# The tail of a two-layer decoder trunk: row factors with one tensor input, products of rows on GpSimd, scaling on VectorE

## The chip, the cores and the metric

The kernel runs on one core of a Trainium2 chip. The metric is the device time of one execution in microseconds; a median of three runs is given, and one further execution was recorded by the hardware profiler. Lower is better.

## The reference, cut to what matters

The program is a decoder trunk of two layers for 512 positions of 1024 features, in float32. Both layers are a mixer and a gated feed-forward block, each behind an RMS norm and added to the residual. After the second feed-forward block comes a last RMS norm:

```python
def rms_norm(x, g):
    x32 = x.astype(jnp.float32)
    y = x32 * lax.rsqrt(jnp.mean(x32 * x32, axis=-1, keepdims=True) + EPS)
    return y.astype(x.dtype) * g
...
    h = h + gated_conv_ffn(hn, w_ffn_gate[layer], w_ffn_up[layer], conv_ffn[layer],
                           b_conv_ffn[layer], w_ffn_down[layer])
return rms_norm(h, final_norm)
```

Only the end matters here: the last part of the down projection of layer 1, the residual `y` that it is added to, and the last norm, which scales each position by a factor of its own and each feature by `final_norm`.

## The kernel before, in words

Matrices in float32 are multiplied as three products of split operands (a high and a low part). In the body of the kernel activations lie with features on the partitions; in the last down projection that turns round, and the output is built as four *rows*: tiles `y[0]` to `y[3]` of 128 positions by 1024 features, each with a left and a right half of 512 features.

The tail is the end of the function `ffn1`. The last four blocks of hidden features are multiplied with their weights by a scheme of seven block products in place of eight (numbers 1 to 7; products 1, 2, 3 and 6 belong to rows 0 and 1, products 5, 7 and 4 to rows 2 and 3). Sums of products share PSUM banks: 1, 6, 7 and 4 go on top of each other in bank "a", 5 and 3 in bank "e", 2 has bank "b"; a product that goes on top of another may start only when VectorE has read the sum so far. The last product of all, number 2 for row 1, is made in two parts of 256 columns in banks "c" and "d".

From `taken(1, 0, left)` on, the order in which VectorE, ScalarE and GpSimd work is written out by hand, line by line: each call is bound to program order (`inorder`), and each engine works through its own instructions in that order. The calls are:

- `taken` (its add has line 1104, its matmuls 1204): makes a block product on TensorE and adds it on VectorE to a half of `y`, times the factor of the feed-forward norm. Inputs of the add: PSUM, a column, `y` in SBUF.
- `squared` (1221): ScalarE squares a half of `y` and writes the sum of squares of each position into a column of `ssf` (an ACTIVATE and a read-out of the accumulator).
- `halved` (1227 for the first half, 1229 for the next): VectorE collects the sums of a row, times -0.5/1024, in another column of `ssf`.
- `rooted` (1232): ScalarE takes the square root.
- `inverted` (1236 to 1238): VectorE takes the reciprocal and improves it by one Newton step of two instructions; the result is the row's factor, one number per position.
- `times` (1241): the product of a half of `y` with `final_norm` (the tile `fin`), on VectorE or GpSimd, into `yf`. It doesn't need the factor.
- `scaled` (1245 on ScalarE, 1246 on GpSimd or VectorE): multiplies `yf` by the factor into `y`, and issues the store of that half (1247; 256 KB), on the queue of SP or, for row 1 right, of ScalarE.
- The last: row 1 left is multiplied by factor and `final_norm` in one VectorE instruction (1307) and stored (1309).

The rows are finished in the order 0, 2, 3, 1. Before the change GpSimd has four instructions in this part: the product of row 2 right, the scaling of row 2 right, the product of row 3 left, the scaling of row 3 left. VectorE makes the other products, except that of row 1 left, which is in the last instruction.

Of the kernel before, what the change touches and what calls it, by code (L numbers as in the profile page):

```python
# [12 lines left out]
ALU = mybir.AluOpType  # L13
# [3 lines left out]
D = 1024  # L17
# [5 lines left out]
EPS = 1e-6  # L23
# [8 lines left out]
def tile_trunk(ctx: ExitStack, tc: tile.TileContext, x, norm_mix, norm_ffn, final_norm,  # L32
# [19 lines left out]
    inorder = tc.keep_in_program_order  # L52
# [1026 lines left out]
    def ffn1(norm):  # L1079
        with tc.tile_pool(name="f1", bufs=1) as ap:  # L1080
# [20 lines left out]
            left, right = slice(0, 512), slice(512, D)  # L1101

            def add(dst, ps, t):
                return nc.vector.scalar_tensor_tensor(dst, ps, ffn.cols[:, t : t + 1], dst,  # L1104
                                                      op0=ALU.mult, op1=ALU.add)
# [86 lines left out]
            def product(p, i, c0=0, c1=512, bank=None):  # L1192

                at = bank or BANK[p], i
                first = at not in banks
                if first:
                    banks[at] = mm_bank(f"dn{a}_{at[0]}{i}")
                ps = banks[at][:, c0:c1]
                cs = slice(i * P, (i + 1) * P)
                (l_hi, l_lo), (r_hi, r_lo) = blocks[p], stat[p]  # L1200
                for k in range(2):
                    for l, r, end in ((l_hi, r_hi, False), (l_hi, r_lo, False),
                                      (l_lo, r_hi, k == 1)):
                        nc.tensor.matmul(ps, l[:, k, cs], r[:, k, c0:c1], start=first, stop=end,
                                         skip_group_check=True)
                        first = False
                return ps

            vec, act, pool = nc.vector, nc.scalar, nc.gpsimd
# [3 lines left out]
            def taken(p, i, cs, bank=None):  # L1213

                t = i + 2 * (p in (5, 7, 4))
                part = cs if bank else slice(0, 512)
                inorder(add(y[t][:, cs], product(p, i, part.start, part.stop, bank), t))

            def squared(t, cs):
                sq = tp.tile([P, S], F32, tag="sq", name=f"sqf{t}_{cs.start}")  # L1220
                inorder(act.activation(sq[:, : cs.stop - cs.start], y[t][:, cs], AF.Square,
                                       accum_out=ssf[:, t, cs.start // 256 : cs.start // 256 + 1]))

            def halved(t, cs, first):

                ss, ms = ssf[:, t, cs.start // 256 : cs.start // 256 + 1], ssf[:, t, 3:4]
                inorder(vec.tensor_scalar(ms, ss, -0.5 / D, -0.5 * EPS, op0=ALU.mult, op1=ALU.add)
                        if first else
                        vec.scalar_tensor_tensor(ms, ss, -0.5 / D, ms, op0=ALU.mult, op1=ALU.add))

            def rooted(t):
                inorder(act.activation(root[t], ssf[:, t, 3:4], AF.Sqrt, scale=-2.0))

            def inverted(t):
                ms, r = ssf[:, t, 3:4], factor[t]
                inorder(vec.reciprocal(r, root[t]))
                inorder(vec.scalar_tensor_tensor(ms, ms, r, r, op0=ALU.mult, op1=ALU.mult))
                inorder(vec.scalar_tensor_tensor(r, ms, 1.5, r, op0=ALU.add, op1=ALU.mult))

            def times(engine, t, cs):  # L1240
                inorder(engine.tensor_tensor(rows_f[t][:, cs], y[t][:, cs], fin[:, cs], ALU.mult))

            def scaled(engine, t, cs, queue=nc.sync):
                dst, src, r = y[t][:, cs], rows_f[t][:, cs], factor[t]
                inorder(act.activation(dst, src, AF.Copy, scale=r) if engine is act else
                        engine.tensor_scalar(dst, src, r, None, op0=ALU.mult))
                queue.dma_start(out[t * P : (t + 1) * P, cs], dst)
# [6 lines left out]
            squared(0, left)  # L1254
            times(vec, 0, left)
            halved(0, left, True)
            taken(6, 0, right)
            taken(6, 1, right)
            taken(3, 0, right)
            squared(0, right)  # L1260
            times(vec, 0, right)
            taken(7, 0, right)
            halved(0, right, False)
            rooted(0)
            squared(2, right)
            times(pool, 2, right)
            inverted(0)
            taken(7, 1, right)
            scaled(act, 0, left)
            scaled(act, 0, right)  # L1270
            halved(2, right, True)
            taken(4, 0, left)
            squared(2, left)
            times(vec, 2, left)
            halved(2, left, False)
            rooted(2)
            taken(5, 1, right)
            squared(3, right)
            inverted(2)
            taken(4, 1, left)  # L1280
            scaled(act, 2, left)
            scaled(pool, 2, right)
            halved(3, right, True)
            times(vec, 3, right)
            times(pool, 3, left)
            squared(3, left)
            taken(3, 1, right)
            squared(1, right)
            halved(3, left, False)
            rooted(3)  # L1290

            first, second = slice(0, 256), slice(256, 512)
            taken(2, 1, first, "c")
            squared(1, first)
            halved(1, right, True)
            taken(2, 1, second, "d")
            squared(1, second)
            inverted(3)
            scaled(pool, 3, left)
            times(vec, 1, right)  # L1300
            halved(1, first, False)
            halved(1, second, False)
            rooted(1)
            scaled(act, 3, right)
            inverted(1)
            scaled(act, 1, right, nc.scalar)
            inorder(vec.scalar_tensor_tensor(y[1][:, left], y[1][:, left], factor[1],
# [4 lines left out]
    n = ffn0(n)  # L1312
    n = mixer1(n)
    ffn1(n)


# [28 lines left out]
```

## Time and profile before

| | |
|---|---|
| median of 3 runs | 988.8 us (988.59 to 989.36) |
| the profiled execution | 988.85 us |
| its span | 987.1 us |
| granted TensorE clock, mean | 0.998 |
| last matmul of the kernel starts | 977.52 us |
| last instruction on VectorE (line 1307) | 981.68 us, 0.75 us long |
| stores of the output | 8 of 256 KB, seven on SP's queue, one on ScalarE's |

The span runs from the first to the last event in the profile; all times of the trace count from its start. In the timeline each row has its start, its length, engine, line of the kernel, operation, and output <- inputs with their shapes; a bracket names the idle time before it and what ended that. VectorE's instructions overlap a little: the next one that depends on nothing begins somewhat ahead of the end that the row shows. In the chain of waits a row has start, length, engine, tile and line.

### The profile page before, as it was taken

The numbers are of one execution on the slowest core, as the hardware profiler recorded it, in microseconds if no ns is written. First come the engines' busy times: TensorE is split into PE (matmuls) and PEld (weight loads), VectorE is DVE, ScalarE is ACT, GpSimd is POOL, SyncE is SP. The second block draws the span as 40 slices with busy tenths as digits, with TensorE's granted clock in tenths as the row PEclk, the third lists the DMA queues.
The fourth block names the chain that finished last, engine by engine and source line by source line (L and its number), as shares of the span: only waits on it lengthen the run. The fifth ranks groups of instructions, "written<-read, shape, count | busy, mean of one in ns | idle before, by whom it ended". The sixth has DMA issues, their size and how long they took to land.

```text
span 987.1 us, 15485 instructions
## 1 busy us (share of the span) xinstructions
PE 975.2 (99%) x6099; PEld 879.9 (89%) x6099; DVE 775.9 (79%) x1181; ACT 562.0 (57%) x843; POOL 112.0 (11%) x129
## 2 busy tenths in 40 slices
PE   9999999999999999999999999999999999999996
PEld 6788888999999999999889988889999999999985
DVE  5797458998788887886887765589987779777787
ACT  5623347755465654655488734576655456554675
POOL 2142022000000000000210001210000000000022
PEclk9999999999999999999999999999999999999999
DMA  7442225555465454653324623264565465445573
GB/s 248 131 150 85 86 86 128 135 137 157 129 150 133 132 142 129 150 130 108 126 64 120 198 69 106 55 140 128 150 166 133 130 149 147 119 135 135 161 151 116
DMA packets 87942, 129.32 MB, mean 131 GB/s; under 512 B 4309, under 2 KB 57789, under 8 KB 87869
## 3 DMA queue, kind: packets, MB, share of 16 engines
q1 hardware_dynamic: 78172, 98.69, 32.2%
q0 software_dynamic: 8208, 27.79, 15.5%
q10 hardware_dynamic: 1488, 1.84, 0.6%
q8 instruction: 48, 0.79, 0.3%
q14 instruction: 26, 0.20, 0.1%
HBM read 98.42 MB, written 2.10 MB: 102 GB/s over the span
## 4 chain that ended last, share of the span: by engine, by line
PE 85%; DVE 8%; ACT 2%; issue 1%; DMA 0%; POOL 0%; ACTq 0%; DVEq 0%
PE dn L153 3%; PE dn L154 3%; PE dn L155 3%; PE d L153 3%; PE d L154 3%; PE d L155 3%; PE oo L155 1%; PE oo L153 1%; PE oo L154 1%; PE oe L154 1%; PE oe L153 1%; PE oe L155 1%; PE u_20a L542 1%; PE u_18a L542 1%; PE u_16a L542 1%
## 5 line engine op out<-in xcount | busy, mean ns | idle before, releaser
L576 DVE SCALAR_TENSOR_TENSOR c<-rows,prm,c 128x512 f32<-128x512 f32 x88 | 64.1, 747 | 1.5 <-ACT c L574 1.4
L140 POOL DMA_DIRECT2D wlo_g<-raw_g x20 | 17.2, 859 | 387.4 <-ACT wlo_g L139 350.4
L153 PE MATMUL d<-a_hi,whi_d 128*128 128x512 f32 x144 | 56.1, 390 | 0.0
L153 PE MATMUL dn<-whi_dn,a_hi 128*128 128x512 f32 x144 | 56.1, 390 | 0.0
L154 PE MATMUL dn<-wlo_dn,a_hi 128*128 128x512 f32 x144 | 56.1, 390 | 0.0
L154 PE MATMUL d<-a_lo,whi_d 128*128 128x512 f32 x144 | 56.1, 390 | 0.0
L155 PE MATMUL d<-a_hi,wlo_d 128*128 128x512 f32 x144 | 56.0, 389 | 0.0
L155 PE MATMUL dn<-whi_dn,a_lo 128*128 128x512 f32 x144 | 56.0, 389 | 0.0
L679 DVE TENSOR_TENSOR wlo_s34u<-s34u,whi_s34u 128x1024 fp32r<-128x1024 f32 x20 | 24.5, 1224 | 25.5 <-ACT whi_s34u L678 25.5
L149 DVE TENSOR_TENSOR wlo_dn<-raw_dn,whi_dn 128x1024 fp32r<-128x1024 f32 x18 | 22.0, 1225 | 23.6 <-ACT whi_dn L148 23.4
L142 ACT ACTIVATE whi_u<-raw_u 128x1024 fp32r<-128x1024 f32 x21 | 22.2, 1055 | 31.6 <-PE d L154 17.5
L149 DVE TENSOR_TENSOR wlo_d<-raw_d,whi_d 128x1024 fp32r<-128x1024 f32 x18 | 22.0, 1224 | 19.5 <-ACT whi_d L148 19.5
L198 ACT ACTIVATE hgh<-h,prm 128x512 fp32r<-128x512 f32 x24 | 17.3, 722 | 35.1 <-DVE h L309 35.0
L140 POOL DMA_DIRECT2D wlo_u<-raw_u x21 | 18.1, 860 | 162.0 <-ACT wlo_u L139 83.7
L584 ACT ACTIVATE s<-c,prm 128x512 f32<-128x512 f32 x44 | 31.2, 714 | 7.3 <-DVE c L576 7.2
L209 POOL TENSOR_TENSOR ssq_f<-ssq_f,sq_f 128x512 f32<-128x512 f32 x14 | 19.7, 1410 | 132.3 <-ACT sq_f L208 97.5
L260 ACT ACTIVATE a_hi<-s 128x512 fp32r<-128x512 f32 x40 | 25.0, 626 | 15.7 <-PE dn L154 9.9
L199 DVE SCALAR_TENSOR_TENSOR hgl<-h,prm,hgh 128x512 fp32r<-128x512 f32 x24 | 23.2, 965 | 12.0 <-ACT hgh L198 11.9
L155 PEld LDWEIGHTS d<-a_hi,wlo_d 128*128 128x128 f32 x144 | 27.0, 188 | 5.7
L155 PEld LDWEIGHTS dn<-whi_dn,a_lo 128*128 128x128 f32 x144 | 27.0, 188 | 5.7
L1104 DVE SCALAR_TENSOR_TENSOR y<-dn,small,y 128x512 f32<-128x512 f32 x40 | 27.7, 748 | 5.5 <-PE dn L155 5.5
L153 PEld LDWEIGHTS d<-a_hi,whi_d 128*128 128x128 f32 x144 | 27.1, 188 | 5.3
(1489 smaller groups left out, 3762.7 us busy)
## 6 DMA issues: line engine op xcount, KB each, us to landing
raw_g<-in_w_ffn_gate_dram SPq DMA_DIRECT2D x40, 512.0 KB, 3.8
raw_u<-in_w_ffn_up_dram SPq DMA_DIRECT2D x40, 512.0 KB, 3.7
raw_dn<-in_w_ffn_down_dram SPq DMA_DIRECT2D x22, 512.0 KB, 3.6
wlo_u<-raw_u POOLq DMA_DIRECT2D x21, 512.0 KB, 5.7
wlo_g<-raw_g POOLq DMA_DIRECT2D x20, 512.0 KB, 4.6
raw_d<-in_w_ffn_down_dram SPq DMA_DIRECT2D x18, 512.0 KB, 3.7
raw_oe<-in_w_out_even_dram SPq DMA_DIRECT2D x8, 512.0 KB, 3.6
raw_v<-in_w_in_odd_dram SPq DMA_DIRECT2D x8, 512.0 KB, 4.5
```

The costliest lines, as they stand in the source:

```text
L140: nc.gpsimd.dma_start(lo, raw, accum_op=ALU.add)
L149: behind(nc.vector.tensor_tensor(lo, raw, hi.bitcast(F32), ALU.subtract), after[0])
L153: nc.tensor.matmul(ps, lhs[0], rhs[0], start=start, stop=False)
L154: nc.tensor.matmul(ps, lhs[0], rhs[1], start=False, stop=False)
L155: nc.tensor.matmul(ps, lhs[1], rhs[0], start=False, stop=stop)
L199: nc.vector.scalar_tensor_tensor(hg[k][1], h[k], g, hg[k][0].bitcast(F32), op0=ALU.mult, op1=ALU.subtract)
L260: nc.scalar.activation(hi, src, AF.Copy, scale=scale)
L542: nc.tensor.matmul(ps, l, r, start=first, stop=end, skip_group_check=True)
L576: nc.vector.scalar_tensor_tensor(c, t[:, i : S + i], prm("cf", i * NF + ft), c, op0=ALU.mult, op1=ALU.add)
L584: nc.scalar.activation(s, c, AF.Silu, bias=self.prm("bf", ft))
L679: nc.vector.tensor_tensor(lo, src, hi.bitcast(F32), ALU.subtract)
L1104: return nc.vector.scalar_tensor_tensor(dst, ps, ffn.cols[:, t : t + 1], dst, op0=ALU.mult, op1=ALU.add)
```

## The change

The columns and the order of the tail are changed, and nothing ahead of it.

- `halved` for the second sum of a row, and both instructions of the Newton step, become `tensor_scalar`: one tensor input of 128x1, and what was the second tensor input is now a scalar operand, a column with one number per partition. The arithmetic is the same.
- Row 2: GpSimd makes both products; ScalarE scales the right half, VectorE the left. Before, VectorE and GpSimd made one product each, ScalarE scaled the left half and GpSimd the right.
- Row 3: GpSimd makes both products; VectorE scales the left half, GpSimd the right. Before, VectorE and GpSimd made one each, GpSimd scaled the left half and ScalarE the right.
- Row 1: GpSimd makes the product of the right half, in place of VectorE. The left half is squared in one instruction of 512 columns and not two of 256, so that there are two sums for the row and not three.
- The order of calls moves with that. Row 3's factor is worked out between the two adds of row 1 left, and row 3's scaling comes ahead of row 1's last sum. On TensorE one matmul of the last product (bank "c") now stands ahead of product 3 of row 1; all else there is as before.

On GpSimd there are now six instructions: the products of row 2 right, row 2 left, row 3 right, row 3 left and row 1 right, then the scaling of row 3 right. The stores keep their order on SP's queue by rows (0, 2, 3, then 1 left), with row 2's right half ahead of its left one as before. Within row 3 the order as the scheduler writes it is the right half (GpSimd's) and then the left (VectorE's); before the change it was the left (GpSimd's) and then the right (ScalarE's). Lines of the changed kernel from 1229 on stand one lower up to 1246 (the sums are all line 1227, the Newton step 1235 to 1237, products 1240, scalings 1244 and 1245), and the last instruction is line 1303.

```diff
--- before.py
+++ after.py
@@ -1224,9 +1224,8 @@
             def halved(t, cs, first):
 
                 ss, ms = ssf[:, t, cs.start // 256 : cs.start // 256 + 1], ssf[:, t, 3:4]
-                inorder(vec.tensor_scalar(ms, ss, -0.5 / D, -0.5 * EPS, op0=ALU.mult, op1=ALU.add)
-                        if first else
-                        vec.scalar_tensor_tensor(ms, ss, -0.5 / D, ms, op0=ALU.mult, op1=ALU.add))
+                inorder(vec.tensor_scalar(ms, ss, -0.5 / D, -0.5 * EPS if first else ms,
+                                          op0=ALU.mult, op1=ALU.add))
 
             def rooted(t):
                 inorder(act.activation(root[t], ssf[:, t, 3:4], AF.Sqrt, scale=-2.0))
@@ -1234,8 +1233,8 @@
             def inverted(t):
                 ms, r = ssf[:, t, 3:4], factor[t]
                 inorder(vec.reciprocal(r, root[t]))
-                inorder(vec.scalar_tensor_tensor(ms, ms, r, r, op0=ALU.mult, op1=ALU.mult))
-                inorder(vec.scalar_tensor_tensor(r, ms, 1.5, r, op0=ALU.add, op1=ALU.mult))
+                inorder(vec.tensor_scalar(ms, ms, r, r, op0=ALU.mult, op1=ALU.mult))
+                inorder(vec.tensor_scalar(r, ms, 1.5, r, op0=ALU.add, op1=ALU.mult))
 
             def times(engine, t, cs):
                 inorder(engine.tensor_tensor(rows_f[t][:, cs], y[t][:, cs], fin[:, cs], ALU.mult))
@@ -1271,37 +1270,34 @@
             halved(2, right, True)
             taken(4, 0, left)
             squared(2, left)
-            times(vec, 2, left)
+            times(pool, 2, left)
             halved(2, left, False)
             rooted(2)
             taken(5, 1, right)
             squared(3, right)
+            times(pool, 3, right)
             inverted(2)
             taken(4, 1, left)
-            scaled(act, 2, left)
-            scaled(pool, 2, right)
+            scaled(act, 2, right)
             halved(3, right, True)
-            times(vec, 3, right)
+            scaled(vec, 2, left)
             times(pool, 3, left)
             squared(3, left)
             taken(3, 1, right)
-            squared(1, right)
+            times(pool, 1, right)
             halved(3, left, False)
             rooted(3)
-
-            first, second = slice(0, 256), slice(256, 512)
-            taken(2, 1, first, "c")
-            squared(1, first)
+            squared(1, right)
+
+            taken(2, 1, slice(0, 256), "c")
+            inverted(3)
+            taken(2, 1, slice(256, 512), "d")
+            squared(1, left)
             halved(1, right, True)
-            taken(2, 1, second, "d")
-            squared(1, second)
-            inverted(3)
-            scaled(pool, 3, left)
-            times(vec, 1, right)
-            halved(1, first, False)
-            halved(1, second, False)
+            scaled(vec, 3, left)
+            scaled(pool, 3, right)
+            halved(1, left, False)
             rooted(1)
-            scaled(act, 3, right)
             inverted(1)
             scaled(act, 1, right, nc.scalar)
             inorder(vec.scalar_tensor_tensor(y[1][:, left], y[1][:, left], factor[1],
```

## The prediction

> **What bounds the kernel now.** The page's list of busy time comes first, to see where the change can matter at all.
>
> ```profile
> span 987.1 us, 15485 instructions
> PE 975.2 (99%) x6099; PEld 879.9 (89%) x6099; DVE 775.9 (79%) x1181; ACT 562.0 (57%) x843; POOL 112.0 (11%) x129
> ```
>
> TensorE (PE) fills nearly the whole span, and the edit leaves its work alone but for one matmul that moves. So only the tail can change, where TensorE runs out of products. The second view is the chain that ended last, cut to the end.
>
> ```profile
> 970.62 0.86 DVE ssf L1237
> ...
> 977.28 0.95 DVE ssf L1229
> ...
> 979.60 0.60 DVE yf L1241
> ...
> 980.38 0.40 DVE ssf L1229
> ```
>
> Its last 14 us are VectorE (DVE) nearly throughout. Two of its pieces, 0.86 and 0.95 us, are instructions on one number per partition. The third view, the timeline, says why.
>
> ```profile
> 970.17 1.29 POOL L1241 TENSOR_TENSOR yf<-y,fin 128x512 f32<-128x512 f32 x1 [7.03 <-DVE ssf L1229]
> ...
> 970.42 0.16 DVE L1236 RECIPROCAL ssf<-ssf 128x1 f32<-128x1 f32 x1 [0.27 <-ACT ssf L1232]
> ...
> 970.62 0.85 DVE L1237 SCALAR_TENSOR_TENSOR ssf<-ssf 128x1 f32<-128x1 f32 x1
> ...
> 975.39 1.57 POOL L1246 TENSOR_SCALAR y<-yf,ssf 128x512 f32<-128x512 f32 x1 [3.93 <-DVE ssf L1238]
> ...
> 975.76 0.14 DVE L1227 TENSOR_SCALAR ssf<-ssf 128x1 f32<-128x1 f32 x1
> ...
> 976.54 0.74 DVE L1104 SCALAR_TENSOR_TENSOR y<-dn_e,small,y 128x512 f32<-128x512 f32 x1
> ...
> 976.94 1.27 POOL L1241 TENSOR_TENSOR yf<-y,fin 128x512 f32<-128x512 f32 x1
> ...
> 977.20 1.03 DVE L1229 SCALAR_TENSOR_TENSOR ssf<-ssf 128x1 f32<-128x1 f32 x1
> ```
>
> L1237 started 0.45 us into a GpSimd (POOL) product and ended with it (971.47 against 971.46); L1229 likewise (978.23 against 978.21). Both read two SBUF tensors. What did not wait beside GpSimd reads one: the reciprocal (0.16), L1227 (0.14), and L1104, whose other tensor is in PSUM (0.74).
>
> After the last VectorE instruction come the stores. The windows of 0.25 us show their transfers (last two columns: DMA share, GB/s).
>
> ```profile
> 982.25:982.50 0.25, 0.00 (x0) 0.00 (x0) 0.18 (x1) 0.15 (x1) 0.00 (x0) 0.78 0.11 41
> 982.50:982.75 0.25, 0.00 (x0) 0.00 (x0) 0.00 (x0) 0.00 (x0) 0.00 (x0) 0.50 0.95 360
> ...
> 985.25:985.50 0.25, 0.00 (x0) 0.00 (x0) 0.00 (x0) 0.00 (x0) 0.00 (x0) 0.50 0.15 49
> ```
>
> Transfers run without a gap from about 982.47 to 985.29: four of 256 KB, 0.70 us each. They are row 3's two halves and row 1's two, the first of them row 3 left: SP's queue, which takes its stores in order, had it waiting until GpSimd had scaled it (981.63, below). From the last byte to the end of the span are 1.81 us, and from the span to the time of this execution (988.85) 1.75; both I leave as they are. The execution is 0.05 over the median, 988.8.
>
> **The change, step by step.** More rows carry the terms.
>
> ```profile
> 971.60 0.39 PE L1204 MATMUL dn_a<-whi_dnp,hgl 128*128 128x512 f32 x1
> ...
> 972.30 0.74 DVE L1104 SCALAR_TENSOR_TENSOR y<-dn_a,small,y 128x512 f32<-128x512 f32 x1
> ...
> 974.32 0.39 PE L1204 MATMUL dn_a<-whi_dnp,hgl 128*128 128x512 f32 x1
> 974.71 0.19 PEld L1204 LDWEIGHTS dn_e<-whi_dnp,hgh 128*128 128x128 f32 x1 [0.43 <-DVE y L1104]
> ...
> 975.97 0.39 PE L1204 MATMUL dn_e<-whi_dnp,hgl 128*128 128x512 f32 x1
> ...
> 977.37 0.63 ACT L1221 ACTIVATE sqf<-y 128x512 f32<-128x512 f32 x1 [0.67 <-DVE y L1104]
> ...
> 977.91 0.19 ACT L1221 ACTIVATION_READ_ACCUMULATOR sqf<-y 128x1 f32 x1
> ...
> 978.61 0.47 DVE L1104 SCALAR_TENSOR_TENSOR y<-dn_d,small,y 128x256 f32<-128x256 f32 x1
> ...
> 979.80 1.83 POOL L1246 TENSOR_SCALAR y<-yf,ssf 128x512 f32<-128x512 f32 x1 [1.59 <-ACT sqf L1221]
> 980.12 0.65 DVE L1229 SCALAR_TENSOR_TENSOR ssf<-ssf 128x1 f32<-128x1 f32 x2
> ...
> 981.23 0.22 DVE L1237 SCALAR_TENSOR_TENSOR ssf<-ssf 128x1 f32<-128x1 f32 x1
> 981.48 0.16 DVE L1238 SCALAR_TENSOR_TENSOR ssf<-ssf 128x1 f32<-128x1 f32 x1
> 981.68 0.75 DVE L1307 SCALAR_TENSOR_TENSOR y<-y,ssf,fin 128x512 f32<-128x512 f32 x1
> 982.43 0.39 ACTq L1247 DMA_DIRECT2D out_dram<-y  x1
> ```
>
> *The small steps.* With one tensor input they should no longer wait for GpSimd. In the rows a small step that needs the one before it starts 0.03 after that one's end (981.45 to 981.48), a big add 0.66 after the add ahead of it. No row has a 128x1 TENSOR_SCALAR with a column as scalar. L1237, which has one, takes 0.22, L1238 without 0.16: so a column is worth 0.06. Bounds are 0.14 (L1227) and 0.28 (two columns at 0.06 more); I take 0.22 for every one, which costs 0.06 twice in each row's chain.
>
> *Row 0.* L1237's wait of 0.63 (0.85 for 0.22) goes. With a column in the sum ahead the reciprocal starts at 970.48, the steps at 970.67 and 970.92, and the next add, of row 3 left, which waits for none of them, at 971.03: 0.55 earlier (the 0.63, less 0.06 for the sum's column and some 0.02 of spacing). Then TensorE is late: the product for row 2 left ends at 971.60 + 0.39 = 971.99, so that add starts at 972.03 (972.30 before). Of 0.55, 0.27 is left.
>
> *Row 2.* VectorE's product of row 2 left goes to GpSimd, which is idle there. VectorE gains nothing at once, as the sum waits for ScalarE (ACT): the square starts at 972.80, its read-out ends 0.73 later (977.37 to 978.10 in the row), the sum runs 973.56 to 973.77. The add of row 3 right ends at 974.44. TensorE, which waited 0.43 for that add, also has one narrow matmul of the last product to run ahead of it now; product 3 starts at 974.67 for 974.71 and, as it no longer breaks at its start, ends at 976.19 for 976.36.
>
> *Row 2 scaled on VectorE.* The form is known from the first mixer, alone and beside a GpSimd product:
>
> ```profile
> 71.59 0.49 DVE L270 TENSOR_SCALAR cv<-rows,prm 128x512 f32<-128x512 f32 x1
> ...
> 74.31 1.04 DVE L270 TENSOR_SCALAR cv<-rows,prm 128x512 f32<-128x512 f32 x1
> ```
> ```profile
> 73.79 1.29 POOL L498 TENSOR_TENSOR cv<-cv,rstd_m 128x512 f32<-128x512 f32 x1 [9.88 <-PE av L155]
> ```
>
> It takes 0.49 alone, and ends 0.27 after the product (75.35 against 75.08) where it has to wait. Here it is asked for at 975.66 (behind row 2's small steps and row 3's left add, which starts at 974.93, plus 0.66, plus 0.07 for a small sum), GpSimd's product of row 3 right runs 974.53 to 975.81, so it ends at 976.09: before product 3 does. Hidden, with 0.1 us to spare.
>
> *Row 3.* The add of row 1 right starts at 976.23 (976.54), row 3's sum 0.66 later and ends at 977.10, where L1229 ended at 978.23: 1.13 us. Root to 977.33, reciprocal to 977.56, two steps: the factor is there at 978.05 (979.60, where the product behind it starts in the chain). The last add, behind the second step, starts at 977.97 for 978.61.
>
> *Row 1.* The two 256-wide squares become one 512-wide: 978.47 to the read-out's end at 979.20 (a price of 0.2). The product of row 1 right (L1241, 0.60 of the chain) is off VectorE, one sum is gone, and the sum of 0.40 that waited beside GpSimd's scaling is free: it runs 979.23 to 979.44, where it ended at 980.77. Then root (0.20), reciprocal (0.16) and two steps (0.22), each with its 0.03: the factor at 980.37, the last instruction 980.40 to 981.15, against 981.68 to 982.43. That is 1.28 us.
>
> *Stores.* SP's queue takes them in its own order. By the order of the instructions row 3 right, which GpSimd scales, now stands ahead of row 3 left, which VectorE scales: so row 3 left, ready at 978.8, waits behind GpSimd, and the last burst has four transfers again. GpSimd scales row 3 right after its product of row 1 right (977.24 to 978.52, behind that of row 3 left, 976.09 to 977.24: 1.27 less a start that the wait covers) and VectorE's scaling of row 3 left (to 978.8); its two rows give 1.57 and 1.83, the second with some 0.4 behind a VectorE product, so I take 1.5: ready at 980.3, against 981.63 for the store that opened the burst before. First bytes come some 0.85 after that (982.47 for 981.63): 981.15. Four transfers of 0.70 end at 983.97. Row 1's stores, issued 0.75 and some 0.8 after the last instruction starts (981.68 to 982.43 before), so at 981.13 and 981.2, have first bytes due at 981.98 and 982.05, and their turns come at 982.55 and 983.25: they have slack of 0.57 and 1.2. So of VectorE's 1.28 nothing reaches the end by itself; what counts is that GpSimd is done 1.33 earlier, thanks to work ahead of it that came earlier or went.
>
> Sum: span 987.1 - 1.3 = 985.8, plus 1.75 makes 987.5. The price of a column does not enter (slack). GpSimd's scaling does, at full: at 1.83 the time is 987.9, at 1.2 (the shortest that I hold possible without a VectorE product beside it, from its 1.57 with one) 987.2. Products at 1.15 for 1.28 would give 0.4 more. So 986.8 to 987.9.
>
> **The Trainium skill, weighed.** Its page "SBUF — State Buffer", section "Who interferes with whom", says that VectorE and GpSimd hold their common pair of ports for a whole instruction, and that `tensor_scalar` may take it in its two-port mode; the L270 row agrees (1.04 for 0.49). Read widely, that speaks against the edit, for the small steps become `tensor_scalar` too; L1227 (0.14 beside GpSimd) is against the wide reading. By the narrow one the sum is 987.5, by the wide one that of the third rival. The section also says that the order of issue decides who waits; it agrees with the rows under the first rival.
>
> **Rivals.** *First: GpSimd gets ahead at a hand-over.* Twice a VectorE scaling waits out a GpSimd product with another GpSimd instruction queued: asked for at 975.66 and 978.43, with the products ending at 975.81 and 978.52. If GpSimd goes on, the scaling, and all VectorE queued behind it, wait for one instruction more.
>
> ```profile
> 55.79 3.47 POOL L484 TENSOR_TENSOR ac<-ac,rstd_m 128x512 f32<-128x512 f32 x2 [0.70 <-DVE pl L464]
> ```
> ```profile
> 56.93 1.19 DVE L262 TENSOR_TENSOR pl_lo<-pl,pl_hi 128x512 fp32r<-128x512 f32 x1
> 58.03 1.78 DVE L456 TENSOR_TENSOR zs<-zs 128x521 f32<-128x521 f32 x1
> ```
>
> Two queued GpSimd products: the VectorE one at 56.93 came in about half a microsecond late, the next waited some 1.1. So VectorE got in between the two. But the margins, 0.15 and 0.09, are the size of my errors. Lost at the second place, GpSimd's scaling is done 0.3 earlier, but row 1's last sum starts at 980.25, 1.0 late: row 1's stores are issued at 982.15, their transfers end at 984.4, time 987.9. Lost at the first, the add of row 1 right starts at 977.26, GpSimd then reaches the second place first too, and row 1's sum starts at 981.15: the last instruction ends at 983.1, the last byte near 985.3, as before: 988.8.
>
> *Second: the products on GpSimd take longer there.* Four follow each other from 972.86 and one scaling.
>
> ```profile
> L484 POOL TENSOR_TENSOR ac<-ac,rstd_m 128x512 f32<-128x512 f32 x4 | 9.7, 2443 | 22.7 <-ACT pl_hi L260 19.0 <-DVE ac L483 3.0 <-DVE pl L464 0.7
> ```
>
> At 2.44 us each the scaling ends at 972.86 + 9.8 + 1.5 = 984.1, or 984.7 with two waits of 0.28 for VectorE. All four transfers follow: 984.7 + 0.85 + 2.8 + 1.81 = 990.2, with 1.75 a time of 991.9, slower than before. It decides where the scaling ends after 981.63, from 1.7 us a product on; from 2.2 the loss passes 0.2%. Against it: L484 ran beside VectorE work on two SBUF tensors; the tail's adds read one, and GpSimd took 1.27 beside one.
>
> *Third: the change doesn't do what it says; the small TENSOR_SCALARs wait too.* Then row 2's factor waits for the product that ends at 975.81, row 3's sum and second step for the next two, row 1's for GpSimd's scaling: the last instruction ends near 984.0, and the time is about 989.7.
>
> **How the numbers follow.** Forecast 0.64, 987.5; second place lost 0.12, 987.9; first place lost 0.08, 988.8; long products 0.10, 988.9 to 991.9; small steps waiting 0.06, 989.7. The range 986.7 to 989.0 holds the first three, the edges of the forecast's own 986.8 to 987.9 included, and the beginning of the fourth. What a measurement here can tell from no change is about 0.2%, 2.0 us: faster by that means under 986.8, the edge of the forecast's case, a quarter of it if I allow for what GpSimd's rows are worth: 0.18. Over 990.8 come only products above 2.2 us: 0.06. Within: 0.76.
>
> **What would show it.** Right: no 128x1 VectorE row over 0.3 us; TENSOR_SCALAR 128x512 on VectorE ends some 0.3 us after a GpSimd product, and before the next; TensorE without its 0.43 us gap; the last burst of four transfers opened by row 3 right, at some 0.85 us behind the end of GpSimd's scaling, with row 1's last instruction long done. Wrong: small rows that end with GpSimd's; GpSimd products well above 1.3 us; GpSimd's scaling of row 3 right ahead of VectorE's of row 3 left; a burst of three.

## The result, and the profile after

| | before | after |
|---|---|---|
| median | 989.09 us (20 runs, 988.49 to 990.14) | 987.58 us (20 runs, 987.10 to 988.79) |
| profiled execution, its span | 988.85, 987.1 | 987.73, 986.0 |

The ratio is 0.9985, with a 95% interval of 0.9979 to 0.9992: faster, by 1.5 us. That is 0.15%, less than the 0.2% that the prediction thought a measurement needed. Forecast were 987.5 and 1.3 us.

First VectorE's rows of the kernel after, from the timeline (start, length, engine, line):

```profile
970.75 0.28 DVE L1236 TENSOR_SCALAR ssf<-ssf 128x1 f32<-128x1 f32 x1
...
974.63 0.27 DVE L1236 TENSOR_SCALAR ssf<-ssf 128x1 f32<-128x1 f32 x1
...
975.78 0.48 DVE L1245 TENSOR_SCALAR y<-yf,ssf 128x512 f32<-128x512 f32 x1
976.32 0.75 DVE L1104 SCALAR_TENSOR_TENSOR y<-dn_e,small,y 128x512 f32<-128x512 f32 x1
976.99 0.20 DVE L1227 TENSOR_SCALAR ssf<-ssf 128x1 f32<-128x1 f32 x1
...
978.58 0.48 DVE L1245 TENSOR_SCALAR y<-yf,ssf 128x512 f32<-128x512 f32 x1
979.46 0.21 DVE L1227 TENSOR_SCALAR ssf<-ssf 128x1 f32<-128x1 f32 x1 [0.40 <-ACT sqf L1221]
...
980.70 0.75 DVE L1303 SCALAR_TENSOR_TENSOR y<-y,ssf,fin 128x512 f32<-128x512 f32 x1
```

and GpSimd's in the same stretch:

```profile
974.60 4.05 POOL L1240 TENSOR_TENSOR yf<-y,fin 128x512 f32<-128x512 f32 x3 [0.37 <-DVE ssf L1235]
978.63 1.87 POOL L1245 TENSOR_SCALAR y<-yf,ssf 128x512 f32<-128x512 f32 x1
```

GpSimd is busy from 974.60 to 980.50 without a break, and no small VectorE step beside it takes over 0.28 us; before, two had taken 0.85 and 1.03. GpSimd's last row is 1.87 long where it takes 1.57 alone (e6): it waited for VectorE's scaling. Row 3's sum (976.99) ends at 977.19, where it had ended at 978.23. Both scalings on VectorE (0.48 each) ran as if alone.

The windows of 0.25 us show the last burst (last two columns DMA share and GB/s):

```profile
981.25:981.50 0.25, 0.00 (x0) 0.00 (x0) 0.20 (x1) 0.25 (x1) 0.00 (x0) 1.00 0.47 180
981.50:981.75 0.25, 0.00 (x0) 0.00 (x0) 0.00 (x0) 0.00 (x1) 0.00 (x0) 0.61 1.05 385
...
984.00:984.25 0.25, 0.00 (x0) 0.00 (x0) 0.00 (x0) 0.00 (x0) 0.00 (x0) 0.50 0.63 221
984.25:984.50 0.25, 0.00 (x0) 0.00 (x0) 0.00 (x0) 0.00 (x0) 0.00 (x0) 0.50 0.10 41
```

Four transfers again. A window counts a packet where it starts; by the single packets of the trace they run from 981.37 (0.86 after GpSimd's scaling) to 984.38, and then it is 1.64 us to the end of the span (before: to 985.42, then 1.72). And here is the chain that ended last, as the profile draws it:

```profile
979.71 0.21 ACT ssf L1231
...
980.45 0.23 DVE ssf L1237
...
980.78 0.72 ACT y L1244
```

It runs through row 1's factor to ScalarE's last scaling and does not know GpSimd or the queue of stores. The prediction said that these last instructions have slack and that GpSimd's scaling sets the end.

Chain and timeline also leave out the closing instructions of the program. The view of the program's last line lists them; these are its rows for GpSimd's DRAIN, an instruction that GpSimd runs three times there, before and then after (shortest, median and longest in ns, then where the first and the last start):

```profile
L1341 POOLq DRAIN  x3: 34/93/6617, 979.8 to 986.9; - x3
```
```profile
L1337 POOLq DRAIN  x3: 34/102/6862, 978.4 to 985.8; - x3
```

The longest of the three is the first. By the trace's records, after the change it ends at 985.24, 4.74 us after GpSimd's last instruction; before it ended at 986.37, also 4.74 after. SP, which waits for the stores to land, is through at 985.03 (before: 986.33), and the span ends at 986.02 (987.13): both times 0.77 after the DRAIN. So there are two ways by which GpSimd's scaling can reach the end, the stores behind it and this DRAIN. Which of them counts, and that the drawn chain does not, the experiments show.

### The profile page after: what moved, and what is told of

The parts are those of the page before. It is cut to its first block, busy times and chain, and to the rows that moved or that the text cites. A ratio compares the mean times of both kernels' runs of the same rounds, so it can differ in the third digit from the quotient of the medians.

```text
span 986.0 us, 15484 instructions
## 1 busy us (share of the span) xinstructions
PE 974.6 (99%) x6099; PEld 879.9 (89%) x6099; DVE 772.8 (78%) x1179; ACT 560.8 (57%) x840; POOL 115.1 (12%) x131
## 4 chain that ended last, share of the span: by engine, by line
PE 86%; DVE 7%; ACT 3%; issue 2%; DMA 1%; POOL 0%; ACTq 0%; DVEq 0%
PE dn L154 3%; PE dn L153 3%; PE dn L155 3%; PE d L154 3%; PE d L153 3%; PE d L155 3%; PE oo L155 1%; PE oo L154 1%; PE oo L153 1%; PE oe L155 1%; PE oe L154 1%; PE oe L153 1%; PE u_20a L542 1%; PE u_16a L542 1%; PE u_14a L542 1%
```

## The experiments

The tail begins earlier or later from one execution to the next (from 968.84 in e5 to 970.57 in e6), so places in it are compared as distances from one event, the mark: the start of VectorE's add of row 2's first right half (line 1104; 969.34 before, 969.42 after), ahead of which no kernel differs. The first five columns of numbers are worked out so from the traces, in us. "Stores landed" is where SP is through with its waits for the stores, "DRAIN ends" is GpSimd's. The last two columns are the measured medians against the kernel before on the same chip.

| kernel | GpSimd's scaling ends | last VectorE instruction starts | stores landed | DRAIN ends | end of span | median (before) | ratio (95%) |
|---|---|---|---|---|---|---|---|
| before | 12.29 | 12.34 | 16.99 | 17.03 | 17.80 | | 1 |
| after | 11.09 | 11.28 | 15.62 | 15.83 | 16.60 | 987.58 (989.09) | 0.9985 (0.9979 to 0.9992) |
| e1: small steps alone | 11.88 | 11.92 | 16.57 | 16.62 | 17.38 | 988.46 (989.44) | 0.9989 (0.9980 to 0.9998) |
| e2: all but the small steps | 12.80 | 13.33 | 17.32 | 17.54 | 18.30 | 989.46 (989.44) | 1.0003 (0.9994 to 1.0011) |
| e3: other order of stores | 11.01 | 11.28 | 15.16 | 15.75 | 16.52 | 987.76 (989.44) | 0.9985 (0.9976 to 0.9994) |
| e4: one product twice | 12.32 | 11.28 | 17.30 | 17.07 | 18.05 | 989.60 (989.44) | 1.0001 (0.9992 to 1.0010) |
| e5: row 3 all on VectorE | none | 11.28 | 15.16 | 13.96 | 15.90 | 987.16 (989.37) | 0.9976 (0.9967 to 0.9985) |
| e6: e3, two squares | 10.77 | 11.31 | 15.04 | 15.51 | 16.27 | 987.48 (989.37) | 0.9982 (0.9973 to 0.9990) |
| e7: GpSimd first | 10.77 | 11.71 | 15.59 | 15.51 | 16.34 | 987.34 (989.37) | 0.9979 (0.9970 to 0.9988) |
| e8: e1, sum later | 11.57 | 11.62 | 16.27 | 16.32 | 17.08 | 988.27 (989.37) | 0.9989 (0.9980 to 0.9998) |
| e9: after, again | 11.08 | 11.28 | 15.61 | 15.82 | 16.59 | 987.74 (989.15) | 0.9986 (0.9977 to 0.9995) |
| e10: e5, again | none | 11.28 | 15.17 | 13.96 | 15.92 | 987.00 (989.15) | 0.9979 (0.9970 to 0.9988) |
| e11: row 3 right on ScalarE, two squares | none | 11.11 | 14.75 | 13.97 | 15.50 | 986.37 (989.15) | 0.9973 (0.9963 to 0.9984) |

The last instruction on VectorE stands at 11.28 in six rows, to the hundredth: the distances repeat far better than the medians, whose intervals are some 0.9 us to each side. Two things hold in every row. The DRAIN ends 4.74 after GpSimd's last instruction (in e5, e10 and e11 that is a product, which ends at 9.22 or 9.23). The span ends 0.75 to 0.77 after the later one of stores and DRAIN. That is the DRAIN in the kernel before, the changed kernel, e1, e2, e3, e6, e8 and e9, by 0.04 to 0.59; in e4, e5, e7, e10 and e11 it is the stores.

### e1 and e2: the two halves of the change

e1 is the kernel before with this alone:

```diff
-                inorder(vec.tensor_scalar(ms, ss, -0.5 / D, -0.5 * EPS, op0=ALU.mult, op1=ALU.add)
-                        if first else
-                        vec.scalar_tensor_tensor(ms, ss, -0.5 / D, ms, op0=ALU.mult, op1=ALU.add))
+                inorder(vec.tensor_scalar(ms, ss, -0.5 / D, -0.5 * EPS if first else ms,
+                                          op0=ALU.mult, op1=ALU.add))
...
-                inorder(vec.scalar_tensor_tensor(ms, ms, r, r, op0=ALU.mult, op1=ALU.mult))
-                inorder(vec.scalar_tensor_tensor(r, ms, 1.5, r, op0=ALU.add, op1=ALU.mult))
+                inorder(vec.tensor_scalar(ms, ms, r, r, op0=ALU.mult, op1=ALU.mult))
+                inorder(vec.tensor_scalar(r, ms, 1.5, r, op0=ALU.add, op1=ALU.mult))
```

e2 is the changed kernel with these lines put back.

> The kernel before with one part of the change alone: the second sum and the two Newton instructions with one tensor input; products, scalings and order of calls as before. Theory A (the gain is the ports: small steps no longer wait for GpSimd, so GpSimd gets row 3's factor earlier and its scaling, which opens the last burst of four stores, is done earlier): row 3's factor near 978.7, GpSimd's scaling of row 3 left done near 980.5 for 981.63, first byte near 981.4, time 987.7, as good as the whole change. Theory B (the gain comes from taking products of rows off VectorE): no more than half of the gain, 988.4 or above. Both: no small step over 0.3 us.

> The changed kernel with the small steps as they were before, with two tensor inputs; products, scalings and order as changed. Theory A: each small step that falls beside a GpSimd product waits for its end (row 2's near 1.3 us, row 3's sum and step, row 1's scaling behind GpSimd's), row 1's last instruction ends near 984.2, time near 989.9, some 1 us slower than the kernel before. Theory B: most of the gain stays, 988.0 or less.

e1's timeline, VectorE and then GpSimd:

```profile
977.80 0.15 DVE L1227 TENSOR_SCALAR ssf<-ssf 128x1 f32<-128x1 f32 x1 [0.34 <-ACT sqf L1221]
...
978.89 0.68 DVE L1240 TENSOR_TENSOR yf<-y,fin 128x512 f32<-128x512 f32 x1
979.49 0.53 DVE L1227 TENSOR_SCALAR ssf<-ssf 128x1 f32<-128x1 f32 x2
```
```profile
979.17 1.83 POOL L1245 TENSOR_SCALAR y<-yf,ssf 128x512 f32<-128x512 f32 x1 [1.29 <-DVE ssf L1237]
```

No small step waits for GpSimd any more, but the time saved meets two other things. VectorE, now early, stands 0.34 us before row 1's first sum, since ScalarE has not read out the square, and row 3's factor is queued behind that. Then VectorE's own product of row 1 right (978.89) starts ahead of GpSimd's scaling, which takes 1.83. So the scaling ends at 11.88: 0.4 earlier than before, where the whole change brings 1.2, and the span follows by the same 0.4. The medians say 1.0 of 1.5 us, with their 0.9 to each side. Theory A was too simple: the ports are not all of it.

e2, VectorE and GpSimd:

```profile
971.30 0.85 DVE L1237 SCALAR_TENSOR_TENSOR ssf<-ssf 128x1 f32<-128x1 f32 x1
...
975.87 1.28 DVE L1237 SCALAR_TENSOR_TENSOR ssf<-ssf 128x1 f32<-128x1 f32 x1
...
981.41 0.80 DVE L1246 TENSOR_SCALAR y<-yf,ssf 128x512 f32<-128x512 f32 x1
```
```profile
975.85 1.29 POOL L1241 TENSOR_TENSOR yf<-y,fin 128x512 f32<-128x512 f32 x1 [0.75 <-DVE ssf L1236]
...
981.25 1.57 POOL L1246 TENSOR_SCALAR y<-yf,ssf 128x512 f32<-128x512 f32 x1 [0.42 <-DVE ssf L1238]
```

Five small steps now wait (0.85, 0.59, 1.28, 0.57, 0.73 long), one of them through a whole product: 975.87 to 977.15 beside 975.85 to 977.14. GpSimd's scaling ends 0.5 later than before, the time is the same as before within 0.9 us (expected: 1 us slower, which the span, 0.5 more, half bears out). Theory B falls: without the small steps the moves bring nothing. The whole gain needs both.

### e3 and e4: what sets the end of the changed kernel

```diff
-                queue.dma_start(out[t * P : (t + 1) * P, cs], dst)
+                put_out = queue.dma_start(out[t * P : (t + 1) * P, cs], dst)
+                if t == 3:
+                    inorder(put_out)
```

> The changed kernel with the store of row 3 left (VectorE's) put ahead of that of row 3 right (GpSimd's) on SP's queue. Theory C (the end is the burst of four transfers that GpSimd's scaling opens, and row 1's last instructions have some 0.4 us of slack against it): three transfers in the last burst, the end set by row 1's two, last byte near 983.75 for 984.2, time 0.4 less than the changed kernel's 987.6. Theory D (the end is row 1's chain on VectorE and ScalarE, as the profile's chain of waits ends): no change, 987.6.

e3 binds row 3's two stores to program order, so that the left half's goes first. It did what it should for the stores, which have landed 0.46 earlier. The median is 1.7 under the kernel before, for 1.5 of the changed one: 0.2 less, which cannot be told from nothing. The trace decides where the median can't. GpSimd's scaling ends only 0.08 earlier, so does its DRAIN, and the span ends 0.08 earlier:

```profile
L1339 POOLq DRAIN  x3: 34/102/6786, 978.5 to 985.8; - x3
```

So in the changed kernel the burst of stores, which theory C names, is not what ends last; neither is row 1's chain of theory D, as e4 shows.

```diff
             scaled(vec, 3, left)
+            times(pool, 1, right)
             scaled(pool, 3, right)
```

> The changed kernel with GpSimd's product of row 1 right made twice, so that its scaling of row 3 right comes some 1.3 us later and nothing on VectorE or ScalarE has to wait. Theory C: first byte of the last burst 1.3 us later, time 1.3 more than the changed kernel's 987.6. Theory D: row 1's last instructions end where they did (981.5), time 987.6.

e4, GpSimd, VectorE, the windows and the queue:

```profile
974.30 5.58 POOL L1240 TENSOR_TENSOR yf<-y,fin 128x512 f32<-128x512 f32 x4 [0.37 <-DVE ssf L1235]
979.88 1.57 POOL L1245 TENSOR_SCALAR y<-yf,ssf 128x512 f32<-128x512 f32 x1
```
```profile
980.40 0.75 DVE L1304 SCALAR_TENSOR_TENSOR y<-y,ssf,fin 128x512 f32<-128x512 f32 x1
```
```profile
982.00:982.25 0.25, 0.00 (x0) 0.00 (x0) 0.00 (x0) 0.00 (x0) 0.00 (x0) 0.50 0.54 197
```
```profile
q10 hardware_dynamic: 112, 0.23, 76.6%
```

VectorE's last instruction starts at the same 11.28, but the span ends 1.45 later and the median is 1.6 more. Nothing that the drawn chain names has moved, so theory D is out: GpSimd's scaling sets the end. It ends 1.23 later, and its DRAIN with it. The last line is from the view of DMA queues (packets, MB, share of the time) for 981.9 to 982.7: the packets there are all of ScalarE's queue (q10), so row 1 right now goes first. The stores on SP's queue begin behind it, at 982.77, and land last, 0.23 after the DRAIN. In e4, then, GpSimd's scaling reaches the end by the stores, in the changed kernel by the DRAIN.

### e5 to e8: the slack, the hand-over, and what e1 lacked

e5 is e3 with `scaled(vec, 3, right)` for `scaled(pool, 3, right)`. e6 is e3 with row 1 left squared in two pieces:

```diff
+            squared(1, slice(0, 256))
             taken(2, 1, slice(256, 512), "d")
-            squared(1, left)
+            squared(1, slice(256, 512))
             halved(1, right, True)
+            halved(1, slice(0, 256), False)
             scaled(vec, 3, left)
             scaled(pool, 3, right)
-            halved(1, left, False)
+            halved(1, slice(256, 512), False)
```

e7 is the changed kernel with VectorE's scaling put last:

```diff
-            scaled(vec, 3, left)
             scaled(pool, 3, right)
             halved(1, left, False)
+            scaled(vec, 3, left)
```

e8 is e1 with `halved(1, right, True)` moved behind `inverted(3)`.

> The changed kernel with row 3 left's store first on SP's queue, as before, and VectorE scaling both halves of row 3, so that GpSimd makes only products. Theory C (the last burst that GpSimd's scaling opens sets the end, row 1's chain is 0.4 us behind it): both stores of row 3 are moved before row 1's factor is there, two transfers in the last burst, end set by row 1's chain, 0.2 to 0.4 us less than the changed kernel. Theory D (row 1's chain already sets the end): no change. The second scaling takes the 0.40 us in which VectorE waits for ScalarE's read-out, so the last sum starts no later than 0.05 us after it did.

> The changed kernel with row 3 left's store first on SP's queue and row 1 left squared in two pieces of 256, the first sum collected ahead of VectorE's scaling. Row 1's last sum starts near 0.3 us earlier. Theory C: now row 1's chain is what ends last, so last byte 0.6 us earlier than in the changed kernel, time 0.6 less (some 0.9979 of before). Theory D: 0.3 less (0.9982).

> The changed kernel with VectorE's scaling of row 3 left put behind row 1's last sum, so that GpSimd's scaling of row 3 right gets the ports first: the hand-over of the first rival, lost on purpose at the second place. If GpSimd's one-input scaling holds the ports to its end, VectorE's scaling, asked for some 0.9 us into it, ends 0.27 us after it (0.7 us long or more), row 1's reciprocal starts some 0.4 us late; GpSimd's scaling is done 0.4 earlier; time within 0.2 of the changed kernel. If GpSimd holds them only while it reads (some 0.5 us), VectorE's scaling takes its 0.48, row 1's chain is late by 0.1, and the time is 0.3 less than the changed kernel.

> The kernel of the first run (the kernel before with small steps of one tensor input) with row 1's first sum, which kept VectorE waiting 0.34 us for ScalarE's read-out, put behind row 3's factor. Theory E (that wait, new there, is why the small steps alone gave only part of the gain): row 3's factor 0.35 us earlier, GpSimd's scaling of row 3 left and the first byte of the last burst 0.3 us earlier, time 0.3 less than the first run (0.9986 of before). If the rest of the gain needs VectorE's product of row 1 right to go, which takes the ports ahead of GpSimd's scaling: the scaling still takes 1.83, and some 0.4 us stays missing against the changed kernel.

e5 and its repetition e10 show what GpSimd's late scaling cost. e10, VectorE and the windows:

```profile
978.63 0.87 DVE L1245 TENSOR_SCALAR y<-yf,ssf 128x512 f32<-128x512 f32 x2
979.51 0.21 DVE L1227 TENSOR_SCALAR ssf<-ssf 128x1 f32<-128x1 f32 x1
```
```profile
981.25:981.50 0.25, 0.00 (x0) 0.00 (x0) 0.25 (x1) 0.25 (x1) 0.00 (x0) 1.00 0.39 140
...
982.25:982.50 0.25, 0.00 (x0) 0.00 (x0) 0.00 (x0) 0.00 (x0) 0.00 (x0) 0.50 0.49 188
```

Two scalings fit into the time in which VectorE waits for ScalarE's read-out, and the sum behind them (979.51, 10.04 from the mark) stands where it stood in the changed kernel (979.46, 10.04). Row 3's transfers end at 981.49, row 1's two begin at 982.36 on their own. The stores have landed 0.44 to 0.46 earlier, as the slack of 0.4 said; the span ends 0.67 to 0.70 earlier, which is some 0.2 more. That is the "something else" of e10's expectation: with GpSimd's last instruction at 9.22 its DRAIN is over at 13.96 and out of the way, where it had come 0.21 after the stores.

e6 lost its gain at a hand-over. VectorE and GpSimd:

```profile
980.05 0.68 DVE L1245 TENSOR_SCALAR y<-yf,ssf 128x512 f32<-128x512 f32 x1
980.66 0.20 DVE L1227 TENSOR_SCALAR ssf<-ssf 128x1 f32<-128x1 f32 x1
```
```profile
979.77 1.57 POOL L1245 TENSOR_SCALAR y<-yf,ssf 128x512 f32<-128x512 f32 x1
```

With one more sum ahead of it VectorE's scaling came to its turn after GpSimd's, and took 0.68 for 0.48; the last sum stands at 10.09, no earlier than in the changed kernel. So neither theory's number for row 1 could come out. The stores have landed 0.58 earlier, most of it by their order, as in e3; the span ends 0.33 earlier, as GpSimd's scaling, which went first, and its DRAIN end 0.32 earlier.

e7 has the same meeting later in GpSimd's scaling:

```profile
980.09 0.88 DVE L1245 TENSOR_SCALAR y<-yf,ssf 128x512 f32<-128x512 f32 x1
980.89 0.14 DVE L1235 RECIPROCAL ssf<-ssf 128x1 f32<-128x1 f32 x1
```
```profile
979.12 1.57 POOL L1245 TENSOR_SCALAR y<-yf,ssf 128x512 f32<-128x512 f32 x1
```

Started 0.97 into it, VectorE's scaling ended 0.28 after its end (980.97 against 980.69). GpSimd is done 0.32 earlier than in the changed kernel, row 1's last instruction starts 0.43 later, the stores have landed where they had (15.59 for 15.62): the first of the two expectations. With the DRAIN earlier it is the stores that end last, and the span ends 0.26 earlier; the median, 0.9979, is lower still, within its interval.

e8 moved what it should: GpSimd's scaling ends 0.30 earlier than in e1, the span 0.3 earlier; the median did not show it (0.9989 both). Theory E holds in the trace for its part. Against the changed kernel 0.5 is still missing, as expected, but not for the expected reason:

```profile
978.56 0.21 DVE L1237 TENSOR_SCALAR ssf<-ssf 128x1 f32<-128x1 f32 x1
```
```profile
978.98 1.89 POOL L1245 TENSOR_SCALAR y<-yf,ssf 128x512 f32<-128x512 f32 x1 [0.93 <-DVE ssf L1227]
```

The scaling took 1.89 beside VectorE's product of row 1 right, but it takes 1.87 in the changed kernel too. What differs is its start, 9.69 from the mark for 9.21. Row 3's factor is ready at 9.48, for 8.79: in e8 its steps stand behind both of VectorE's last adds, in the changed kernel between them. How much the product of row 1 right costs by itself, no run tells.

### e9 to e11: the base again, and a better version

> The changed kernel itself, as a base beside the next two on one chip: 0.9985 of the kernel before.

> The kernel with both halves of row 3 scaled on VectorE, a second time beside the changed kernel. Theory C (the changed kernel's end is set by the burst that GpSimd's scaling opens; without it row 1's chain sets it, 0.4 us sooner): 0.4 us under the changed kernel, some 0.9981 of before, and row 1's last instruction at the same distance from the tail's start as there. If the 0.7 to 0.9 us seen in the first look hold, something else is saved too: 0.9976.

```diff
-            scaled(pool, 3, right)
...
             rooted(1)
+            scaled(act, 3, right)
```

This, on e6, is e11.

> Row 3 left scaled on VectorE and stored first, row 3 right on ScalarE while it waits for row 1's factor, row 1 left squared in two pieces: GpSimd makes only products, and VectorE's scaling has no GpSimd scaling beside it (which had cost 0.20 us and the whole gain of the two pieces). Theory C: row 1's last sum some 0.2 us earlier than with both halves on VectorE, row 1's last instruction 0.2 us earlier, time 0.2 under that kernel and 0.6 under the changed one. Theory D (nothing but row 1's chain counts): 0.2 under the changed kernel.

e11, VectorE and ScalarE:

```profile
978.63 0.48 DVE L1245 TENSOR_SCALAR y<-yf,ssf 128x512 f32<-128x512 f32 x1
979.03 0.21 DVE L1227 TENSOR_SCALAR ssf<-ssf 128x1 f32<-128x1 f32 x1
```
```profile
979.38 0.70 ACT L1244 ACTIVATE y<-yf,ssf 128x512 f32<-128x512 f32 x1
980.32 0.72 ACT L1244 ACTIVATE y<-yf,ssf 128x512 f32<-128x512 f32 x1 [0.24 <-DVE ssf L1237]
```

Without GpSimd beside it the scaling takes 0.48 again, the last sum is at 9.88 (0.16 earlier), and ScalarE's scaling of row 3 fits in while it would wait for row 1's factor, with 0.24 to spare. The changed kernel came out as in its 20 runs. e11 is the fastest of all: 986.37, 2.8 us under the kernel before and 1.4 under the changed one on the same chip; the intervals of e11 and e9 overlap, but the spans (15.50 for 16.59) and all medians go the same way. That is more than either theory said. Of the 0.42 by which the span is shorter than e10's, 0.17 is there at VectorE's last instruction; the rest came in the stores, and why is open.

## Why the prediction was right

The time came out as forecast, and the step that decided was named: GpSimd's scaling, not the drawn chain. The path from that scaling to the end was only half right (see "The end"). Where a place of the changed kernel is compared with the one worked out, the 0.08 by which this tail started later is taken off.

- **The small steps.** Right that they no longer wait: 0.14 to 0.28 beside GpSimd, so the wide reading and the third rival fall. The price of a column is 0.06, as taken: one column 0.20 or 0.21, but two 0.27 or 0.28, the stated upper bound, where 0.22 was taken for all. Row 1's last instruction came 0.22 later than worked out (980.62 for 980.40): some 0.15 by the two-column steps of rows 3 and 1, and 0.07 as ScalarE began row 1's square 0.10 after the add, where 0.03 was taken. It cost nothing, since it had slack.
- **TensorE.** Product 3's first matmul at 974.66 for 974.67, its end at 976.20 for 976.19; the gap of 0.43 is gone.
- **The two hand-overs.** Won, both. At the second, VectorE's scaling began at 978.58 and GpSimd's next instruction at 978.63: the margin that was put at 0.09. In e6 GpSimd went first there, and VectorE's scaling took 0.20 longer. The first rival's 1.0 us was too dear, as it took GpSimd's scaling to hold VectorE up from its beginning to its end. The rule weighed in the prediction, that the ports are held for a whole instruction, does not fit e2 and e6 either. The first place was not tried.
- **Long products.** Did not come: 1.27 to 1.30, and 1.54 for the one behind VectorE's scaling.
- **Small steps that wait.** Did not come in the changed kernel; e2 shows their price with two tensor inputs, 0.5 us of span against the kernel before and 1.7 against the changed one.
- **The end.** GpSimd's scaling was worked out to end at 980.3 and ended at 980.42, the span at 985.8 and 985.9. The burst came as described, 0.86 behind it, though row 1's last instruction was not yet done when it opened. But the prediction let the end hang on this burst and a fixed 1.81 from the last byte on, for which it gave no reason, and the traces show another term in its place: GpSimd's DRAIN, 4.74 after the scaling, and 0.77 from there. Before, the two paths lay 0.04 apart. In the changed kernel the stores came 1.37 earlier, the DRAIN and the span 1.20. Both paths begin at the same scaling, so the forecast by the one fits the other; that much of the agreement is luck.
- **Slack.** The slack of row 1's stores was put at 0.57 and 1.2. Row 1 left's was issued at 981.48, its first bytes were due 0.83 later (as in e5), at 982.31, and came at 982.76: 0.45. e5 and e10 bear that out.
- **What the prediction did not say:** how the gain divides. Small steps alone would have brought a part, the moves alone nothing (e1, e2).

What stays open: why the DRAIN takes 4.74 us, and whether it depends on the instruction ahead of it; in these runs that was a scaling or a product of 128x512, with the same 4.74.

## What to carry to other kernels

When VectorE's small instructions wait for GpSimd, first take the second tensor input out of those that stand in a chain: then work for GpSimd can be placed beside them, which before cost as much as it gave (e2). At the end of a kernel look beyond the drawn chain, at the queue of stores and at the closing instructions: here GpSimd's last instruction set the end, by its DRAIN or by the store that waited for it, while the chain named others. Let GpSimd's last work end early (e5, e11). Delay one suspect by a known amount (e4) before shortening anything.

## What the runs showed of the hardware

- GpSimd's DRAIN at the end of the program ended 4.74 us after GpSimd's last instruction in all 13 profiles, with that instruction anywhere from 9.22 (e5) to 12.80 (e2) after the mark; the span ended no sooner than 0.75 after it.
- GpSimd's scaling of 128x512 with one tensor input (1.57 alone) is not closed to VectorE all the time: a VectorE scaling that began 0.16 or 0.28 us after GpSimd's start was done 0.96 after that start, at 0.80 and 0.68 long (e2, e6), and GpSimd still took 1.57; one that began 0.97 in waited for GpSimd's end (e7). VectorE's last instruction, with two SBUF tensors, began 0.52 in and took the 0.75 that it takes alone (e4). That GpSimd holds the ports while it reads and again while it writes would fit, but is only argued.
- GpSimd's one-input scaling (1.57) is slower than its product of two tensors (1.29).
